# A fused ReGLU MLP on one core: the verdict's last sum moves from TensorE to GpSimd, and TensorE and VectorE get a closing instruction each before the branch

## The chip, the core and the metric

The kernel runs on one core of one Trainium2 chip. The metric is device time in microseconds (us) of one execution. Besides the time, each run has a span: from the first to the last instruction of the kernel's own program in the profile. The time is about 2 us longer than the span.

## The reference, cut to what matters

```python
# x: 16 x 256 x 512, w1: 512 x 4096, w2: 2048 x 512, all float32 and normally distributed
h = x @ w1
gate, value = np.split(h, 2, axis=-1)
h = np.maximum(gate, 0) * value
return (h @ w2).astype(np.float32)
```

## The kernel before

The kernel has two ways to the result. The fast way uses f16 operands and a scheme with seven products in place of eight for each 2x2 block (P1 to P7). It is safe only for inputs of ordinary size. So, while it runs, other engines collect statistics of all inputs in a tile `st`; near the end a verdict is formed from them, and a branch at the very end either skips the general way or runs it. For these inputs it is always skipped.

```python
    with ExitStack() as fast:
        unfit = fast_way(fast, tc, x2, w1, w2, out2, flag)
    with tc.If(unfit > 0, label="general"):
        with ExitStack() as general:
            general_way(general, tc, x2, w1, w2, out2)
```

The verdict compares each statistic with two bounds, sums over the free dimension on VectorE, sums over the 128 partitions with a matmul of TensorE, and compares the sum on VectorE. Each engine then loads the flag into a register. The kernel also places a hint `LikelyTaken` for this branch on TensorE and VectorE (in the trace one hint instruction on each, at 284.93 and 286.24 us); taken means here that the general way is jumped over.

```python
    def judge():
        n = st.shape[1]
        ok = wpool.tile([P, n], F32, name="ok")
        fit = wpool.tile([P, 2], F16, name="fit")
        nc.vector.tensor_scalar(out=ok, in0=st, scalar1=HIGH, scalar2=None, op0=LE)
        nc.vector.scalar_tensor_tensor(out=ok, in0=st, scalar=LOW, in1=ok, op0=GE, op1=MULT)
        nc.vector.memset(fit, 1.0)
        ...
            nc.vector.tensor_reduce(out=fit[:, :1], in_=ok, axis=mybir.AxisListType.X, op=ADD)
        return fit

    def hint_here():
        ...
        tc.mark_branch_hint_location("general", "LikelyTaken", [ENG.PE, ENG.DVE])
        ...

    def count(fit):
        n = P * st.shape[1]
        ps = psx.tile([P, TH], F32, name="X", tag="X")
        nc.tensor.matmul(ps[:1, :1], fit[:, :1], fit[:, 1:], start=True, stop=True)
        nc.vector.tensor_scalar(out=flag, in0=ps[:1, :1], scalar1=n - 0.5, scalar2=None, op0=LT)

    # in the last second product, which is traced in 112 steps of two matmuls:
            job(18, lambda: verdict.append(judge()))
            job(46, lambda: count(verdict[0]))
            job(78, lambda: verdict.append(nc.values_load(flag[0:1, 0:1], ...)))
            job(40, hint_here)
```

The last product of the whole kernel is P4 of the last pair. ScalarE evicts it from PSUM, and SyncE sends it out:

```python
        def P4(self):
            nc.scalar.activation(self.o[:, 1, :DO // 2], self.Y, COPY, scale=1 / GS)
            self.send(1, slice(0, DO // 2 if self.end else DO))
            if self.t in ((0, 2) if self.s else (0, 1, 2)):
                some_look()
```

## Time and profile before

| kernel before | value |
|---|---|
| time, median of 6 runs | 307.86 us (307.52 to 308.58) |
| span of the profiled run | 305.6 us |
| TensorE busy | 98% |
| end of the last product's last matmul | 302.11 us |
| from there to the end of the span ("the tail") | 3.52 us |

The head of the profile page, the shares of the chain that ended last, and the two queues of the kind "instruction" (packets, MB, share of the DMA engines):

```profile
PE 300.7 (98%) x1933; PEld 187.0 (61%) x1933; DVE 236.0 (77%) x388; ACT 176.5 (58%) x348; POOL 151.2 (49%) x189
...
q8 instruction: 16, 0.26, 0.3%
q14 instruction: 14, 0.11, 0.1%
...
PE 96%; DMA 1%; SPq 0%; POOL 0%; ACT 0%; issue 0%
```

TensorE (PE), busy for 98% of the span and 96% of the chain that ended last, is the bound of this kernel. Another engine can change its time only where TensorE waits for it, or where TensorE has nothing left to do. This is where the counting matmul stands, in the timeline (start, duration, engine, line, operation, in us):

```profile
286.90 0.60 PE L369 MATMUL Y<-v_T,w_stage 128*128 128x256 f16 x4
...
287.43 0.08 PEld L675 LDWEIGHTS <-fit 128*1 128x1 f16 x1 [0.21 <-issue]
287.43 0.16 PE L675 MATMUL X<-fit 128*1 128x1 f16 x1
...
287.53 0.61 PE L369 MATMUL Y<-v_T,w_stage 128*128 128x256 f16 x4
```

Two groups of four matmuls start 0.63 us apart. A full group of eight takes 0.874 us, so four take 0.44: the count costs 0.19 us.

The tail is less plain. The timeline gives the last work of each engine:

```profile
301.08 1.04 PE L369 MATMUL Y<-v_T,g 128*128 128x256 f16 x8
301.28 0.42 DVE L405 SCALAR_TENSOR_TENSOR o<-W,pu 128x256 f32<-128x256 f32 x1 [2.12 <-PE W L369]
302.15 0.38 ACT L417 ACTIVATE o<-Y 128x256 f32<-128x256 f32 x1 [1.36 <-PE Y L369]
```

What the sequencers do is seen only when the branch's line (42) is asked for. A q after an engine's name marks the records of its sequencer; the EVENT_SEMAPHORE is the first instruction that each of the two shows after the jump. The columns are count, shortest/median/longest duration in ns, and first and last start in us:

```profile
L42 PEldq COMPARE_BRANCH  x1: 407/407/407, 300.0 to 300.0; - x1
L42 DVEq COMPARE_BRANCH  x1: 90/90/90, 301.3 to 301.3; - x1
L42 PEldq EVENT_SEMAPHORE  x1: 51/51/51, 302.2 to 302.2; - x1
...
L42 DVEq EVENT_SEMAPHORE  x1: 21/21/21, 304.3 to 304.3; - x1
```

VectorE branches at 301.29 us, as soon as its last instruction has started, and its next instruction comes at 304.26, 2.97 us later. SyncE waits in turn for everything at the end, and a closing barrier of 0.95 us ends the span. Two rows of its waits in the last 7 us (total, times, longest); the rows of earlier outputs and of the closing barrier of all engines are left out:

```profile
SPq L812 <- DVEq L42: 0.3, 1, 0.3
SPq L812 <- DMA out_dram<-o: 0.3, 1, 0.3
```

So SyncE waits for VectorE first, and then a little longer for the last output to land. VectorE's late return is almost hidden, not quite.

### The profile page before, as it was taken

The numbers are of one execution on the slowest core, as the hardware profiler recorded it, in microseconds if no ns is written. First come the engines' busy times: TensorE is split into PE (matmuls) and PEld (weight loads), VectorE is DVE, ScalarE is ACT, GpSimd is POOL, SyncE is SP. The second block draws the span as 40 slices with busy tenths as digits, with TensorE's granted clock in tenths as the row PEclk, the third lists the DMA queues.
The fourth block names the chain that finished last, engine by engine and source line by source line (L and its number), as shares of the span: only waits on it lengthen the run. The fifth ranks groups of instructions, "written<-read, shape, count | busy, mean of one in ns | idle before, by whom it ended". The sixth has DMA issues, their size and how long they took to land.

```text
span 305.6 us, 5338 instructions
## 1 busy us (share of the span) xinstructions
PE 300.7 (98%) x1933; PEld 187.0 (61%) x1933; DVE 236.0 (77%) x388; ACT 176.5 (58%) x348; POOL 151.2 (49%) x189
## 2 busy tenths in 40 slices
PE   8999999999999999999999999999999999999995
PEld 6854545688844444478864444458884444447884
DVE  2779888899768898887537888888546888888851
ACT  2588886455955555538855555545866555553231
POOL 2399999800069999300029989800006998800000
PEclk9999999999999999999999999999999999999999
DMA  7977679954794170001354910000325110000133
GB/s 236 356 233 219 213 176 177 223 114 87 266 200 92 64 138 3 0 2 63 136 175 108 206 36 2 0 2 2 138 91 185 35 34 2 1 1 27 45 105 107
DMA packets 35838, 32.89 MB, mean 108 GB/s; under 512 B 14432, under 2 KB 31328, under 8 KB 35680
## 3 DMA queue, kind: packets, MB, share of 16 engines
q1 hardware_dynamic: 33536, 26.22, 28.7%
q0 software_dynamic: 2272, 6.29, 11.6%
q8 instruction: 16, 0.26, 0.3%
q14 instruction: 14, 0.11, 0.1%
HBM read 27.26 MB, written 12.58 MB: 130 GB/s over the span
## 4 chain that ended last, share of the span: by engine, by line
PE 96%; DMA 1%; SPq 0%; POOL 0%; ACT 0%; issue 0%
PE Y L256 26%; PE W L256 18%; PE X L256 18%; PE Y L369 14%; PE X L369 9%; PE W L369 9%; DMA w_stage<-in_w_dram 1%; PE W L332 1%; PE X L332 1%; PE Y L332 1%; PE Y L511 0%; PE X L511 0%; SPq L501 0%; POOL w_T L479 0%; SPq L222 0%; ACT o L417 0%
## 5 line engine op out<-in xcount | busy, mean ns | idle before, releaser
L256 PEld LDWEIGHTS <-w_T 128*128 128x128 f16 x524 | 51.1, 98 | 54.6 <-POOL w_T L237 0.9
L184 POOL TENSOR_TENSOR fold<-xh 128x1024 f32<-128x1024 f16 x16 | 30.3, 1896 | 94.6 <-DMA xh<-x 93.7
L256 PE MATMUL X<-x_A,w_B 128*128 128x512 f16 x248 | 73.7, 379 | 0.0
L256 PE MATMUL Y<-x_S,w_T 128*128 128x512 f16 x220 | 65.4, 379 | 0.0
L256 PEld LDWEIGHTS <-w_B 128*128 128x128 f16 x372 | 36.4, 98 | 42.0
L284 DVE SCALAR_TENSOR_TENSOR cc<-W,pu 128x512 f32<-128x512 f32 x62 | 42.9, 692 | 21.3 <-ACT pu L278 21.3
L264 ACT COPY Y<-X 128x512 f32<-128x512 f32 x62 | 35.4, 571 | 38.2 <-PE X L256 37.9
L278 ACT ACTIVATE pu<-Y 128x512 f32<-128x512 f32 x62 | 37.1, 598 | 33.9 <-PE Y L256 32.9
L187 POOL TENSOR_TENSOR fold<-fold 128x512 f32<-128x512 f32 (+2 forms) x96 | 51.8, 540 | 7.5
L369 PEld LDWEIGHTS <-w_stage 128*128 128x128 f16 x512 | 50.0, 98 | 5.8
L294 DVE SCALAR_TENSOR_TENSOR cc<-Y,pu 128x512 f32<-128x512 f32 x62 | 42.9, 691 | 6.6
L289 DVE SCALAR_TENSOR_TENSOR g<-X,cc 128x512 f16<-128x512 f32 x62 | 42.9, 691 | 2.3
L306 DVE SCALAR_TENSOR_TENSOR g<-Y,cc 128x512 f16<-128x512 f32 x62 | 42.3, 682 | 1.8 <-PE Y L256 1.8
L369 PEld LDWEIGHTS <-g 128*128 128x128 f16 x384 | 37.5, 98 | 8.2
L271 ACT ACTIVATE pu<-W 128x512 f32<-128x512 f32 x62 | 37.2, 600 | 0.8 <-PE W L256 0.6
L256 PE MATMUL W<-x_S,w_T 128*128 128x512 f16 (+1 forms) x152 | 36.9, 340 | 0.0
L256 PE MATMUL W<-x_S,w_B 128*128 128x512 f16 x124 | 36.9, 379 | 0.0
L256 PE MATMUL Y<-x_A,w_T 128*128 128x512 f16 x124 | 36.9, 379 | 0.0
L369 PE MATMUL X<-w,g 128*128 128x256 f16 x256 | 31.9, 273 | 0.0
L405 DVE SCALAR_TENSOR_TENSOR o<-W,pu 128x256 f32<-128x256 f32 x16 | 6.8, 423 | 21.0 <-PE W L369 21.0
L174 DVE TENSOR_TENSOR w_stage<-g 128x1024 f16<-128x1024 f16 x32 | 21.4, 685 | 0.2
L237 POOL TENSOR_TENSOR w_T<-w_stage 128x512 f16<-128x512 f32 (+1 forms) x16 | 18.7, 1173 | 2.6 <-DMA w_stage<-in_w_dram 2.5
(100 smaller groups left out, 306.7 us busy)
## 6 DMA issues: line engine op xcount, KB each, us to landing
w_stage<-in_w_dram SPq DMA_DIRECT2D x14, 512.0 KB, 6.0
out_dram<-o SPq DMA_DIRECT2D x26, 256.0 KB, 2.2
x<-in_x_dram POOLq DMA_DIRECT2D x4, 1024.0 KB, 10.5
xh<-x SPq DMA_DIRECT2D x16, 256.0 KB, 3.2
w<-in_w_dram POOLq DMA_DIRECT2D x2, 1024.0 KB, 10.0
out_dram<-o SPq DMA_DIRECT2D x12, 128.0 KB, 1.7
w_stage<-in_w_dram SPq DMA_DIRECT2D x4, 256.0 KB, 4.8
x_S<-in_x_dram SPq DMA_DIRECT2D x4, 256.0 KB, 5.7
```

Of the source, the lines that this page charges most:

```text
L174: eng.tensor_tensor(o[n], o[i0], o[i1], op=op)
L184: nc.gpsimd.tensor_tensor(fold, t, t, op=MULT)
L187: nc.gpsimd.tensor_tensor(fold[:, :, :m], fold[:, :, :m], fold[:, :, m:2 * m], op=ADD)
L256: nc.tensor.matmul(ps[:, slice(*c)], wop[wn][:, b, self.jb * P:(self.jb + 1) * P], self.xo[xn][:, b, slice(*c)], start=fresh and b == c[0] ...
L264: nc.scalar.copy(out=self.Y, in_=self.X)
L271: nc.scalar.activation(self.p5, self.W, COPY, scale=GS)
L278: nc.scalar.activation(self.u2, self.Y, COPY, scale=GS)
L284: nc.vector.scalar_tensor_tensor(out=self.c12, in0=self.W, scalar=GS, in1=self.u2, op0=MULT, op1=ADD)
L289: nc.vector.scalar_tensor_tensor(out=self.g[:, self.jb, :TH], in0=self.X, scalar=0.0, in1=self.c12, op0=MAX, op1=MULT)
L294: nc.vector.scalar_tensor_tensor(out=self.c22, in0=self.Y, scalar=GS, in1=self.p5, op0=MULT, op1=ADD)
L306: nc.vector.scalar_tensor_tensor(out=self.g[:, self.jb, TH:], in0=self.Y, scalar=0.0, in1=self.c22, op0=MAX, op1=MULT)
L369: nc.tensor.matmul(ps, self.op[an][:, i], vop[wn][:, i], start=name in ("P1", "P5") and i == 0, stop=i == NJ // 2 - 1, skip_group_check=True)
```

## The change

It takes the counting matmul out of TensorE's stream, since GpSimd is idle by then (its last work ends at 266.9 us). And it makes VectorE and TensorE do one thing more after the last product, so that both reach the branch later.

```diff
         def P1(self):
-            self.Y = psy.tile([P, TH], F32, name="Y", tag="Y")[:, :DO // 2]
+            self.bank = psy.tile([P, TH], F32, name="Y", tag="Y")
+            self.Y = self.bank[:, :DO // 2]
...
         def P4(self):
             nc.scalar.activation(self.o[:, 1, :DO // 2], self.Y, COPY, scale=1 / GS)
             self.send(1, slice(0, DO // 2 if self.end else DO))
+            if self.s == NS - 1 and self.t == NB // 2 - 1:
+                nc.vector.tensor_copy(out=warm_b[:, :DO // 2], in_=self.Y)
+                nc.tensor.matmul(self.bank[:, :P], vop["T4"][:, 0, :P], vop["T4"][:, 0, :P], start=True, stop=True)
...
     def judge():
-        fit = wpool.tile([P, 2], F16, name="fit")
+        fit = wpool.tile([P, 1], F32, name="fit")
...
-        nc.vector.memset(fit, 1.0)
-        with nc.allow_low_precision("whole numbers below 2048"):
-            nc.vector.tensor_reduce(out=fit[:, :1], in_=ok, axis=mybir.AxisListType.X, op=ADD)
+        nc.vector.tensor_reduce(out=fit, in_=ok, axis=mybir.AxisListType.X, op=ADD)
...
     def count(fit):
-        ps = psx.tile([P, TH], F32, name="X", tag="X")
-        nc.tensor.matmul(ps[:1, :1], fit[:, :1], fit[:, 1:], start=True, stop=True)
-        nc.vector.tensor_scalar(out=flag, in0=ps[:1, :1], scalar1=n - 0.5, scalar2=None, op0=LT)
+        total = wpool.tile([1, 1], F32, name="total")
+        nc.gpsimd.tensor_reduce(out=total, in_=fit, axis=mybir.AxisListType.C, op=ADD)
+        nc.gpsimd.tensor_scalar(out=flag, in0=total, scalar1=n - 0.5, scalar2=None, op0=LT)
...
-            job(46, lambda: count(verdict[0]))
+            job(18, lambda: count(verdict[0]))
```

## The prediction

> **What bounds the kernel now.** TensorE. The page's busy line gives PE 98% of a 305.6 us span, and the chain that ended last is 96% PE; the granted clock is 1.000. The last quarter (276 us on) runs second-product groups of eight 128x256 matmuls, one group each 0.874 us, back to back. The other engines wait for it there; GpSimd's last work ends at 266.9 us. So only TensorE's stream and the tail after its last matmul can move the time.
>
> **Removed.** The counting matmul. In the timeline of 286 to 288 us a half group starts at 286.90, the count's weight load at 287.43 after 0.21 us of idle ("issue"), the second half at 287.53. Two halves normally start 0.44 us apart, here 0.63: the count costs 0.19 us on the critical path.
>
> **Moved.** The sum over partitions goes to an idle GpSimd. VectorE's reduce ends at about 284.5 us. TensorE's sequencer loads the flag at 292.6 us, ScalarE's at 293.4, VectorE's at 294.4, and TensorE has about 2 us of matmuls queued at that point. So GpSimd has 8 us before TensorE could starve. [...]
>
> **Added, in the tail.** Before: the last matmul ends at 302.13; ScalarE evicts 302.15 to 302.53; the last output DMA is issued at 302.56 and SyncE's last wait, for its landing, passes at about 304.69. Beside this, VectorE's sequencer takes the branch at 301.29, as soon as its last instruction (waiting for the product before the last) starts, and its next instruction comes only at 304.26, 2.97 us later, though its work ended at 301.70. SyncE waits for that (0.26 us), then 0.3 us more for the DMA. I read the 3 us as an instruction fetch after the taken branch [...]. The spare is about 0.4 us.
>
> The new VectorE copy waits for the last product (302.15), so VectorE's branch moves from 301.29 to about 302.16 and its next instruction to about 305.1. TensorE branched at 300.0, ahead of its queued matmuls; now it waits for the copy (about 0.42 us for 128x256 from PSUM to f16, as early casts of that shape) and for ScalarE, runs 0.1 us, and branches at about 302.65. With the 2.15 us it took before at most, it is back at 304.8; with VectorE's 3 us, at 305.6. SyncE's last wait then passes at about 305.3 instead of 304.69: +0.6 us, up to +1.0 if TensorE's fetch is the later. The output's own path is unmoved.
>
> **Sum.** -0.19 + 0.6 to 1.0: about +0.5 us, 0.2%. Predicted 308.5 us, 8 in 10 between 307.6 and 309.6. Faster by over 2%: 0.01; within 2%: 0.95; slower: 0.04.
>
> **What would show it.** (1) No gap between half groups near 287 us. (2) GpSimd's reduce before about 289 us, TensorE never waiting for the flag. (3) VectorE's branch near 302 us, 3 us to its next instruction. (4) SyncE's last waits ended by VectorE or TensorE, no longer by the DMA. (5) The last eviction still 0.38 us.
>
> **What would make it wrong.** A reduce over 8 us [...] would stall TensorE by the excess. If VectorE's 3 us is not a fetch paid after the branch, the tail stays and the result is 0.2 us faster. If the hint covers one engine [...], the tail may move by a microsecond either way.

The forecast counted the time of GpSimd's sum as hidden: -0.19 us for the count and +0.6 to +1.0 us for the tail came to about +0.5 us, or 308.5 us.

## The result, and the profile after

The changed kernel takes 309.21 us (median of 6 runs, 309.03 to 310.22) against 307.86 us: 1.35 us more. The ratio is 1.0046, with a 95% interval from 1.0026 to 1.0066. Ratios here are the mean time of one kernel's runs over that of the other's runs of the same rounds, so not quite the ratio of the medians. All outputs are right.

TensorE's stream lost the count. The groups of eight now follow each other 0.87 us apart where it stood, and GpSimd's two instructions fit between. The timeline after:

```profile
285.48 0.73 POOL L677 CROSS_LANE_REDUCE total<-fit 128x1 f32<-128x1 f32 x1 [17.55 <-DVE fit L659]
...
286.31 0.50 POOL L678 TENSOR_SCALAR flag<-total 1x1 int32<-1x1 f32 x1
...
286.96 1.04 PE L369 MATMUL W<-v_T,w_stage 128*128 128x256 f16 x8
...
287.83 1.04 PE L369 MATMUL Y<-v_T,w_stage 128*128 128x256 f16 x8
```

The flag is there at 286.81 us and TensorE's sequencer loads it at 293.31, 6.5 us later. From the first matmul of the first block in the seven-product scheme (line 256) to the end of the last product the profiled run takes 286.59 us, against 286.78 before: the 0.19 us is real. The tail, however, grew. The timeline after:

```profile
301.80 1.04 PE L369 MATMUL Y<-v_T,g 128*128 128x256 f16 x8
302.00 0.42 DVE L406 SCALAR_TENSOR_TENSOR o<-W,pu 128x256 f32<-128x256 f32 x1 [2.13 <-PE W L369]
...
302.88 0.38 ACT L418 ACTIVATE o<-Y 128x256 f32<-128x256 f32 x1 [1.36 <-PE Y L369]
303.29 0.42 DVE L421 CAST warm<-Y 128x256 f16<-128x256 f32 x1 [0.86 <-ACT o L418]
303.77 0.22 PE L422 MATMUL Y<-v_T 128*128 128x128 f16 x1 [0.93 <-DVE warm L421]
```

The VectorE copy does not start with ScalarE's eviction at 302.88, but after it: what ended its wait was ScalarE, not TensorE. The branch's line after:

```profile
L42 DVEq COMPARE_BRANCH  x1: 90/90/90, 303.3 to 303.3; - x1
...
L42 PEldq COMPARE_BRANCH  x1: 407/407/407, 303.8 to 303.8; - x1
L42 PEldq EVENT_SEMAPHORE  x1: 51/51/51, 304.2 to 304.2; - x1
L42 DVEq EVENT_SEMAPHORE  x1: 21/21/21, 306.6 to 306.6; - x1
```

TensorE is back 0.47 us after its branch, VectorE 3.27 us after its own. Of SyncE's waits after, this row is for the end of VectorE's jump; that for the landing of the output is gone:

```profile
SPq L814 <- DVEq L42: 2.2, 1, 2.2
```

The tail is 4.83 us (302.84 to 307.67), against 3.52. The two profiled runs should not be subtracted as wholes: their spans, 307.7 and 305.6 us, also differ by 0.92 us in the opening, where weights are still arriving (that first line-256 matmul starts at 16.25 us against 15.33). In the profiles of the other kernels it starts anywhere from 15.4 to 16.2 us (15.40 in e1, which has the verdict on GpSimd, and 15.91 in e2, which has not), so I take that for scatter and not for the change.

### The profile page after: what moved, and what is told of

Its sections match the earlier page's. It is cut to its first block, busy times and chain, and to the rows that moved or that the text cites. A ratio compares the mean times of both kernels' runs of the same rounds, so it can differ in the third digit from the quotient of the medians.

```text
span 307.7 us, 5339 instructions
## 1 busy us (share of the span) xinstructions
PE 300.3 (98%) x1933; PEld 186.5 (61%) x1933; DVE 236.0 (77%) x387; ACT 176.5 (57%) x348; POOL 152.8 (50%) x191
## 4 chain that ended last, share of the span: by engine, by line
PE 96%; DMA 2%; SPq 0%; POOL 0%; DVE 0%; issue 0%; ACT 0%
PE Y L256 26%; PE W L256 17%; PE X L256 17%; PE Y L369 14%; PE W L369 9%; PE X L369 9%; DMA w_stage<-in_w_dram 2%; PE X L332 1%; PE W L332 1%; PE Y L332 1%; PE Y L515 0%; PE X L515 0%; SPq L505 0%; PE Y L159 0%; POOL w_B L483 0%; DVE warm L421 0%
```

## The experiments

Theory A: the whole loss comes from VectorE's late branch. The copy holds the branch back, and after the branch VectorE needs the 3 us that the profiles show (2.97 before, 3.27 after), which I took for a fetch of instructions. Rival B: the closing matmul holds TensorE at the branch. Rival C: the verdict on GpSimd costs time. The spreads of the times are near 1 us, so the tail in each profile is given beside the time. Each group of runs on one chip has its own runs of the kernel before (medians 307.94 to 308.19 us).

| kernel | time, us | ratio to before (95%) | tail, us | VectorE's branch to its next | mean time minus span, us |
|---|---|---|---|---|---|
| before | 307.86 | 1 | 3.52 | 2.97 | 1.8 |
| changed | 309.21 | 1.0046 (1.0026 to 1.0066) | 4.83 | 3.27 | 2.14 |
| e1_gpsimd_only | 307.84 | 1.0009 (0.9987 to 1.0031) | 3.50 | 3.04 | 2.13 |
| e2_closing_only | 309.15 | 1.0039 (1.0026 to 1.0052) | 4.74 | 3.18 | 1.80 |
| e3_copy_only | 309.36 | 1.0046 (1.0032 to 1.0060) | 4.62 | 3.07 | 2.18 |
| e4_matmul_only | 307.89 | 0.9998 (0.9985 to 1.0012) | 3.24 | 2.97 | 2.15 |
| e5_copy_of_w | 308.09 | 0.9999 (0.9984 to 1.0013) | 3.31 | 3.04 | 2.14 |
| e6_short_general | 307.43 | 0.9979 (0.9964 to 0.9994) | 3.10 | 0.63 | 1.77 |
| e7_early_hint | 307.98 | 1.0002 (0.9989 to 1.0015) | 3.15 | 0.63 | 2.15 |
| e8_gpsimd_early_hint | 308.00 | 1.0001 (0.9987 to 1.0015) | 3.53 | 0.63 | 2.18 |
| e9_matmul_early_hint | 307.70 | 0.9992 (0.9980 to 1.0004) | 3.22 | 0.63 | 2.10 |
| e10_no_hint | 310.40 | 1.0070 (1.0054 to 1.0085) | 5.95 | 3.01 | 2.15 |
| e11_fewer_loads | 307.36 | 0.9974 (0.9958 to 0.9991) | 3.12 | 0.63 | 1.78 |

### The parts of the change, one at a time

The first four kernels each keep a part. The closing lines alone removed (e1):

```diff
-            if self.s == NS - 1 and self.t == NB // 2 - 1:
-                nc.vector.tensor_copy(out=warm_b[:, :DO // 2], in_=self.Y)
-                nc.tensor.matmul(self.bank[:, :P], vop["T4"][:, 0, :P], vop["T4"][:, 0, :P], start=True, stop=True)
```

> The changed kernel without its closing copy and matmul: only the verdict on GpSimd is left of the change. Theory A (the whole loss is VectorE's branch, which the copy holds back): 0.2 us faster than the kernel before, since the counting matmul's 0.19 us leaves TensorE's stream; VectorE's branch again about 0.85 us before the last matmul ends, 3.0 us to its next instruction, tail (last matmul's end to the end of the span) 3.5 us. Rival C (the verdict on GpSimd costs time itself, through a late flag or another order): as slow as the changed kernel, +0.5 us or more over before.

The tail is that of before (3.50 us) and the stream is 286.57 us long, 0.2 us shorter than before. The time, however, does not show the 0.2 us: its ratio is 1.0009 with an interval of 0.22% to each side, and one of the six runs took 309.79 us. Rival C as stated (+0.5 us) is not seen in the median, but the gain is not seen either. The reason was found later: it is in the last column of the table.

The closing lines alone added to the kernel before (e2), in the place where the change has them:

```diff
+                nc.vector.tensor_copy(out=warm_b[:, :DO // 2], in_=self.Y)
+                nc.tensor.matmul(self.bank[:, :P], vop["T4"][:, 0, :P], vop["T4"][:, 0, :P], start=True, stop=True)
```

> The kernel before plus the closing copy and matmul alone; the verdict stays on TensorE. Theory A: tail 4.8 us as in the changed kernel, time 1.4 to 1.6 us over before (the changed kernel's loss plus the 0.19 us that the count keeps). Rival C: no slower than before by more than 0.3 us.

The tail is 4.74 us and the loss 0.39%, or 1.2 us. The closing lines alone make the loss of the tail. (I had expected 1.4 to 1.6 us, that is, a whole 0.19 us more than the changed kernel lost. That part is a miss, and again the last column tells why.)

The changed kernel without the matmul (e3), then without the copy (e4):

```diff
-                nc.tensor.matmul(self.bank[:, :P], vop["T4"][:, 0, :P], vop["T4"][:, 0, :P], start=True, stop=True)
```

> The changed kernel without the closing matmul; the VectorE copy stays. Theory A: same as the changed kernel within 0.2 us, 1.2 to 1.5 us over before; VectorE's next instruction about 3.3 us after its branch ends the tail, TensorE branches early. Rival B (the closing matmul holds TensorE at the branch, and that is what ends late): as e1_gpsimd_only, 0.2 us under before.

```diff
-                nc.vector.tensor_copy(out=warm_b[:, :DO // 2], in_=self.Y)
```

> The changed kernel without the VectorE copy; the closing matmul stays and waits for ScalarE's eviction. Theory A: as e1_gpsimd_only, 0.2 us under before (tail 3.5 us), because TensorE comes back within 0.5 us of its branch, before the last output has landed. Rival B: as the changed kernel, 1.0 us or more over before.

The copy alone keeps the loss (1.0046). The matmul alone has none (0.9998; I had expected 0.2 us under before, and the last column tells why that is missing), and its tail, 3.24 us, is even shorter than that of before. Rival B falls.

### Is it the copy, or its wait?

```diff
-                nc.vector.tensor_copy(out=warm_b[:, :DO // 2], in_=self.Y)
+                nc.vector.tensor_copy(out=warm_b[:, :DO // 2], in_=self.W)
```

> The changed kernel, its closing copy reading the product before the last (another bank, ready 0.87 us earlier) in place of the last. Theory A (it is the copy's wait that holds VectorE's branch back): VectorE branches 0.4 to 0.8 us before the last matmul ends, tail 3.2 to 3.4 us, time as the closing matmul alone, 307.9 us. Rival (the copy's own work or the PSUM read costs the time): 309 us, as the changed kernel.

The same copy of another tile, whose product was ready 0.87 us earlier, costs nothing: VectorE branches at 302.01 us, 0.82 us before the last matmul ends, and the tail is 3.31 us. So it is not the copy's work but its wait. The changed kernel's copy of `Y` waits for ScalarE (VectorE's 0.86 us of idle time before it end with ScalarE's eviction), although both only read `Y`: it started at 303.29 us, 0.41 us after that eviction began. No run here lets both read at once, so what that would do is not shown.

### Are the 3 us a fetch?

If VectorE waits for instructions that lie far away, a shorter skipped block should end the wait. The skipped block was cut to one of its eight rounds. That would be wrong for inputs that fail the verdict; these pass.

```diff
-    for c in range(T // TH):
+    for c in range(1):
```

> The changed kernel with the skipped block cut to one of its eight rounds (wrong for inputs that fail the verdict; these pass it), so VectorE's jump spans some 84 instructions in place of some 448. Theory A, fetch form (the 3 us after the branch is a fetch of instructions that lie too far): VectorE's next instruction follows the branch within 0.5 us; the tail is then the last output's landing, 2.9 to 3.3 us; time 307.5 us. Rival (any taken branch of VectorE costs 3 us, whatever the distance): 309.2 us and 3 us from branch to next instruction.

The branch's line of this kernel:

```profile
L42 DVEq COMPARE_BRANCH  x1: 90/90/90, 303.0 to 303.0; - x1
...
L42 DVEq EVENT_SEMAPHORE  x1: 21/21/21, 303.7 to 303.7; - x1
```

VectorE is back 0.63 us after its branch (I had expected under 0.5), the tail falls from 4.83 to 3.10 us, and the time to 307.43 us. With all eight rounds in the block it was 3.27 us (changed), with one it is 0.63, as the fetch theory expects.

But the kernel hints that branch. In the trace of the kernel before, four of the 14 packets of q14 (8 KB each) come 125 to 128 of VectorE's recorded instructions apart; I take these for VectorE's fetches and the rest mostly for other engines'. The last one before the branch is at 268.32 us, and the hint comes at 286.24. (One more q14 packet, at 289.53 us, comes 1.1 us after GpSimd's own jump. It does not fit VectorE's count and is absent in e12, where GpSimd does not jump, so I put it down to GpSimd.) So the hint was moved to the middle of the first product (about 240 us), for VectorE only:

```diff
-        tc.mark_branch_hint_location("general", "LikelyTaken", [ENG.PE, ENG.DVE])
+        tc.mark_branch_hint_location("general", "LikelyTaken", engines)
...
                 getattr(blocks[jb], n)()
+                if (s, n, jb) == (NS - 1, "P1", 4):
+                    hint_here([ENG.DVE])
...
-            job(40, hint_here)
+            job(40, lambda: hint_here([ENG.PE]))
```

> The changed kernel with VectorE's branch hint moved from the last second product to the middle of the first product before it (about 240 us), ahead of the instruction fetch that is seen at about 269 us. Theory A with an ineffective hint (the hint came after the next stretch of code had been fetched, so it fetched nothing): VectorE's next instruction within 0.5 us of the branch, tail 2.9 to 3.3 us, 307.5 us. Rival (the hint's place does not matter[...]): unchanged at 309.2 us.

The branch's line of this kernel, and then two of SyncE's waits at its end:

```profile
L42 DVEq COMPARE_BRANCH  x1: 90/90/90, 303.2 to 303.2; - x1
...
L42 PEldq COMPARE_BRANCH  x1: 412/412/412, 303.6 to 303.6; - x1
L42 DVEq EVENT_SEMAPHORE  x1: 21/21/21, 303.8 to 303.8; - x1
L42 PEldq EVENT_SEMAPHORE  x1: 51/51/51, 304.1 to 304.1; - x1
```

```profile
SPq L816 <- PEq L816: 0.7, 2, 0.5
...
SPq L816 <- DMA out_dram<-o: 0.5, 1, 0.5
```

Nothing of the work has changed, only the hint's place, and the loss is gone: 307.98 us, ratio 1.0002. VectorE is back after 0.63 us although it still branches late, and the last wait of SyncE before the closing barrier (the PEq row) is for the output again. (It was 0.5 us slower than the 307.5 I expected; the last column again.) The page of this kernel has one instruction packet less on q14, 13 in place of 14:

```profile
q14 instruction: 13, 0.11, 0.1%
```

The packets fit a fetch. In all eight profiles with a long jump of VectorE (before, changed, e1 to e5 and e10: 2.97 to 3.27 us) one 8 KB packet of q14 begins 1.02 to 1.44 us after VectorE's branch and has landed 1.3 to 1.5 us before its next instruction. In all five with the 0.63 us jump (e6 to e9 and e11) no packet comes between the two, and the page counts 13. So in these runs the 3 us come with a fetch; its transfer alone is 0.3 to 0.7 us of them, and what fills the rest is not shown.

The counter-test removes all hints from the changed kernel:

```diff
-            job(40, hint_here)
```

> The changed kernel without any branch hint. Theory A with hints that work only ahead of a fetch: VectorE as before, 3.0 to 3.3 us from its branch to its next instruction, because its hint did nothing; TensorE, whose hint did work, now also pays about 3 us in place of 0.47, so its next instruction comes near 306.8 us, beside VectorE's: time 309.2 to 309.6 us. Rival (the hint has no effect on either): TensorE still 0.47 us from branch to next, time 309.2 us.

```profile
L42 DVEq COMPARE_BRANCH  x1: 72/72/72, 303.5 to 303.5; - x1
...
L42 PEldq COMPARE_BRANCH  x1: 3898/3898/3898, 304.0 to 304.0; - x1
L42 DVEq EVENT_SEMAPHORE  x1: 21/21/21, 306.6 to 306.6; - x1
L42 PEldq EVENT_SEMAPHORE  x1: 51/51/51, 308.0 to 308.0; - x1
```

Without hints TensorE pays too: 3.96 us in place of 0.47, more than the 3 us I had expected, and the time is 310.40 us (309.2 to 309.6 expected). The queue q8 has 17 packets in place of 16, one of them inside that wait. (I take q8 for TensorE's: in the kernel before its 16 KB packets come each 118 to 138 recorded matmuls from 135 to 295 us.) VectorE's 3.01 us are the same as with its old hint. So the hint served TensorE and did nothing measurable for VectorE. TensorE's hint (285.86 us in the changed kernel) was followed by an instruction fetch of TensorE (296.22 us) before its branch; VectorE's late hint was followed by no fetch of its own before its branch, its early one by that at 269.12 us. That a hint acts through the next fetch fits all three, but its inner working is argued and not shown.

### What the closing matmul is good for

The e4 tail was 0.28 us shorter than that of before. In the trace, TensorE's instruction fetch after the branch began at 301.92 us in the kernel before, ran for 0.93 us and so met the issue of the last output at 302.56. With the closing matmul (e4) it comes at 304.17. To see whether this is the cause, the verdict on GpSimd with the early hint was run with the closing matmul (e9) and without (e8).

> Verdict on GpSimd and closing matmul, no copy, VectorE's hint early: meant as the fastest. Theory A: VectorE leaves the end of the chain, but the last output's landing lies only 0.1 us behind it there, so 0.0 to 0.2 us under the closing matmul alone: 307.7 us, tail 3.1 to 3.25 us. Rival (VectorE's jump was hiding nothing, or the hint does not work): no change, tail 3.24 us with 3 us from branch to next instruction.

> The verdict on GpSimd and VectorE's hint early, without closing copy and matmul; against e9_matmul_early_hint only the closing matmul is missing. Theory D (with the matmul held back, TensorE's instruction fetch after its branch no longer meets the issue of the last output, whose issue then takes 0.33 us in place of 0.66): issue 0.65 us, tail 3.5 us although VectorE is back early, time 0.2 to 0.3 us over e9_matmul_early_hint, near 307.9 us. Rival (the early hint alone gives the 3.2 us tail): tail 3.2 us, issue 0.33 us, 307.7 us.

The issue of the last output, in SyncE's timeline, first without the matmul and then with it:

```profile
302.72 0.67 SPq L381 DMA_DIRECT2D out_dram<-o  x1
```

```profile
303.10 0.33 SPq L381 DMA_DIRECT2D out_dram<-o  x1
```

Without the matmul the issue takes 0.67 us and the tail is 3.53 us; with it they are 0.33 and 3.22. (Each tail is of one profile; the times, 308.00 and 307.70 us, have overlapping intervals.) The issue is long in every profile where TensorE branches early (before, e1, e3, e8: 0.65 to 0.67 us) and short in every other (0.33). The closing matmul thus wins 0.3 us of the tail by delaying TensorE's branch. VectorE's fetch is not the cause: it overlaps a short issue in e4 and no part of the long one in e3. That it is the overlap of the two transfers, rather than something else about TensorE's early return, is argued from their times and not shown. VectorE's early hint adds nothing measurable to either. Without the matmul (e1) the output lands last anyway. With it (e4) VectorE's return was in fact what SyncE waited for last, but the output had all but landed: with the early hint the tail is 3.22 us in place of 3.24.

### Where the 0.2 us of the count went

The last column of the table explains the misses. The time minus the span is 1.73 to 1.91 us in all runs of the kernel before, and 2.08 to 2.27 us in the runs of the changed kernel and of every experiment with the GpSimd verdict except e6 and e11 (below). That is about 0.33 us outside the span, which no profile shows. The kernels with 1.8 us are those whose compiled GpSimd program is shorter: its last instruction has number 295 in before and e2 and 241 in e6 (seven rounds of eight transfers fewer), but 297 in the others. What VectorE runs did not grow: from before to e1 its executed instructions went from 388 to 386, and GpSimd's from 189 to 191. To test this, e9 was given a general way that loads `w2` and `x` two blocks at a time. This takes 24 instructions from GpSimd (and 8 from VectorE) in the skipped block, and leaves what runs as it was.

```diff
     for h in range(NH):
-        t = xp.tile([P, DO], F32, name="g_t", tag="g_t")
-        nc.gpsimd.dma_start(out=t, in_=w2[h * P:(h + 1) * P, :])
-        nc.vector.tensor_copy(out=w2_sb[:, h], in_=t)
+        if h % 2 == 0:
+            t = xp.tile([P, 2, DO], F32, name="g_t", tag="g_t")
+            nc.gpsimd.dma_start(out=t, in_=w2[h * P:(h + 2) * P, :].rearrange("(a p) n -> p a n", p=P))
+        nc.vector.tensor_copy(out=w2_sb[:, h], in_=t[:, h % 2])
...
-            t = xp.tile([P, D], F32, name="g_t", tag="g_t")
-            nc.gpsimd.dma_start(out=t, in_=x2[c * TH + b * P:c * TH + (b + 1) * P, :])
+            if b % 2 == 0:
+                t2 = xp.tile([P, 2, D], F32, name="g_t", tag="g_t")
+                nc.gpsimd.dma_start(out=t2, in_=x2[c * TH + b * P:c * TH + (b + 2) * P, :].rearrange("(a p) d -> p a d", p=P))
+            t = t2[:, b % 2]
```

> e9_matmul_early_hint with 24 fewer GpSimd instructions in the skipped block (its loads taken two at a time). In all runs so far the time minus the span is 1.8 us for kernels whose GpSimd program ends at instruction 295 or before (before, e2_closing_only, e6_short_general) and 2.1 to 2.2 us for those that end at 297 (the changed kernel and all others). Theory E (the length of GpSimd's program costs 0.33 us after the span): time minus span 1.8 us, span 305.6 us as e9, time 307.4 us, ratio to before 0.998. Rival (the verdict on GpSimd itself costs the 0.33 us outside the span): 2.1 us, 307.7 us.

The difference is back at 1.78 us (1.74 to 1.82, against 2.10 in e9), the median span stays at 305.6 us, and the time is 307.36 us: ratio 0.9974, interval 0.9958 to 0.9991. This is the first kernel that keeps the general way and is faster than the kernel before, clear of noise. So it is the amount of code, skipped code included, and not the running of the GpSimd verdict, that made the 0.33 us. What exactly happens in that time stays open: 24 instructions of GpSimd and 8 of VectorE went together. No trace covers that time, and why two instructions more (295 to 297) should matter is not shown.

As the general way was edited in e11, it was also run once (e12): e11 with the condition turned round:

```diff
-    with tc.If(unfit > 0, label="general"):
+    with tc.If(unfit < 1, label="general"):
```

> The same with the condition of the branch turned round, so that the skipped block runs and overwrites the output: tells only whether the block with the paired loads is right. Expected: correct, some hundreds of us slower.

Its result was correct, in 798.44 us (one run, at a mean granted clock of 0.929).

## Why the prediction was right or wrong, point by point

The measured 309.21 us lies in the predicted range (307.6 to 309.6), within 2% of before as forecast, and the direction was right. The size was not: +0.5 us was predicted, +1.35 us measured. That the range still held it is owed to its width: the copy's wait for ScalarE and the term outside the span, both below, were not foreseen, and both lengthen the time.

- **The count costs 0.19 us in TensorE's stream: right.** The stream is 286.59 us after and 286.78 before.
- **GpSimd's sum is hidden: right.** It took 0.73 us, its comparison 0.50 us, and the flag was 6.5 us early. My forecast of its time was a guess.
- **VectorE's branch is held back and its 3 us then end the kernel: right in mechanism, shown by e3, e5, e6 and e7.** The reading as a fetch fits as well (one q14 packet within each of the eight long jumps and none within the five short ones; 0.63 us in e6), and the forecast that SyncE's last wait would be for an engine and no longer for the output was right.
- **"The new VectorE copy waits for the last product (302.15), so VectorE's branch moves from 301.29 to about 302.16": this step was mis-sized.** I let the copy read `Y` beside ScalarE. It waits until ScalarE has done, 0.41 us more. Against the end of the last matmul the branch moved from -0.82 to +0.47 us, which is 1.29 us and not 0.87. The jump itself was 0.30 us longer in that profile (3.27 against 2.97); over the profiles of e1 to e5 it is 2.97 to 3.18, so I take that part for scatter (its fetch began 1.44 us after the branch, in place of 1.04 before). The last SyncE wait passed 0.15 us after VectorE's return in place of 0.43. The sum, 1.29 + 0.30 - 0.28, is the 1.31 us by which the tail grew; I had 0.6 to 1.0.
- **TensorE's return after 2.15 to 3 us: wrong, without effect.** It took 0.47 us with its hint (3.96 without, e10). The 2.15 us before were its wait for its own queued matmuls: its next instruction came 0.04 us after the last one ended.
- **A term was missing altogether:** 0.33 us between the span and the time, which takes back more than the 0.19 us that the count had given. With it the sum is -0.19 + 1.31 + 0.33 = 1.45 us, beside 1.35 by the medians and 1.42 by the ratio.
- **"If the hint covers one engine": it did.** I named this as a way to be wrong. It was instead what left the 3 us standing, before the change as after: the hint was set for both engines, but only TensorE was faster with it (0.47 us, and 3.96 without any in e10; VectorE 3.27 and 3.01).

## What to carry to other kernels

Read the tail engine by engine and with the sequencers: in the changed kernel VectorE reached the final branch 0.47 us after the last matmul, and the whole of its 3.27 us lay behind it, though no work was left. In these runs a branch hint helped an engine only where a later fetch of that engine came before the branch (0.47 us on TensorE, hint at 285.86 and fetch at 296.22; 0.63 us on VectorE, hint at about 240 and fetch at 269.12; 3.27 us on VectorE with no fetch after the hint), so look for that fetch when placing one; moving VectorE's hint by some 45 us was worth as much as the whole loss here (309.21 to 307.98 us). And look at who else reads a tile: the copy that read the tile of ScalarE's eviction started 0.41 us after it, which counted because VectorE's branch waited behind it.
